# A lead-in with a written order on TensorE: modulation columns amid the products, modulation weights loaded ahead of x, products of zeros first

## The chip, the core and the metric

The kernel runs on one core of a Trainium2 chip. The metric is the device time of one execution in microseconds. A time is given as the median of several executions, and a profile shows one execution of its own. The engines are named as in the profile: PE is TensorE (matrix products), PEld its weight loads, DVE is VectorE, ACT is ScalarE, POOL is GpSimd, and SP is the engine that issues most of the transfers from memory.

## What is computed

One inference step of a two-layer trunk for 512 latent tokens (`x_sample`) and 128 context tokens (`x_prompt`), each a row of 1024 features. Layer 0 is gated attention with grouped keys and values, layer 1 a gated linear recurrence. The change touches the start of layer 0 alone:

```python
def _adaln(cond, w, b):
    mod = silu(cond) @ w + b                  # w: 1024 x 3072
    return split(mod, 3)                      # shift, scale, gate

# layer 0, for the context tokens (cond = c_ctx) and the latent tokens (cond = c)
sh, sc, g = _adaln(cond, ada_w[0], ada_b[0])
h = x * (1.0 + sc) + sh                       # the modulated tokens
proj = h @ attn_w_in                          # q, k, v and the gate path
...
out = attention(q, k, v) * silu(gate) @ attn_w_out
x = layer_norm(ALPHA * x + g * out)
```

So before the first product of a feature's rows of `attn_w_in` can run, three things are wanted: that feature of x with features on the partitions (a transpose), its shift and scale (a small product with 1 MB of `ada_w` for 128 features), and the weights.

## The kernel before

All products are float32 made of three products in a faster format: an operand is split into a high part (a rounded copy, made by ACT) and a low part (the rest, made by DVE), and high x high, high x low and low x high are added up in PSUM. In the names, `hhi` and `hlo` are the parts of the modulated tokens, `kvhi` and `kvlo` those of the key and value columns of `attn_w_in`, and `whi` and `wlo` those of other weights.

The lead-in handles the 1024 features as eight feature tiles of 128, which the text numbers 0 to 7, and the 640 tokens as five token tiles. For one feature tile the steps are:

- **Transposes** (`flip`, lines 440 to 450): TensorE turns x for two feature tiles at once, in ten transposes into three PSUM banks (`xps`, 4, 4 and 2 of them); DVE, ACT and DVE copy them to `h32`.
- **Modulation columns** (`ada_feat`, line 279): 16 products of silu(cond) with two 512 KB pieces of `ada_w` (`raw<-in_ada_m`), eight with each piece, into `adaps`. DVE copies the sum to `row` (line 292), two tiny products on TensorE (`ada_feat_out`, line 286) turn it onto the partitions, and DVE adds the bias, which gives `shsc` (line 287).
- **Modulation** (`modulate`, lines 452 to 458): DVE scales and shifts `h32` (line 455, two instructions), ACT makes `hhi` (line 457), and DVE makes `hlo` (line 458).
- **Key and value products** (`kv_mms`, lines 474 to 476): 15 products of 512 columns, three for each token tile, added up over all eight feature tiles in five PSUM banks (`acc`). Their weights come in four pieces of 512 KB for two feature tiles each (`raw<-in_attn_kv`), which ACT and DVE split (lines 224 and 225).

After the lead-in, 120 products of 256 columns make the first queries (`pmm`, lines 337 to 339), and then the gate path begins (`gps`, line 330). Everything up to the end of attention lies in one scheduled block: a planner with an instruction timeline of its own sets the order of each engine's instructions from the dependencies, and `pin` (`tc.keep_in_program_order`) keeps those so marked in the order in which the code is written. Before the change, `pin` holds only loads and a few others in the lead-in, so that TensorE's order is the planner's. Loads go through one list, `order`, which `pump` issues on SP's queue; the lead-in's pieces share a ring of eight buffers (`RAW_START`), and a load waits until its buffer is read out. `bank1` hands out three PSUM banks in turn, which transposes, modulation sums and the tiny products share.

## Time and profile before

| | us |
|---|---|
| median of 3 runs | 848.7 (845.87 to 850.77) |
| the profiled execution, its own time | 848.41 |
| its span, first to last instruction | 846.6 |
| TensorE busy | 813.1 |
| first gate-path product starts (end of what the change can touch directly) | 73.89 |
| TensorE idle before that point | 9.4 |

Times of rows are microseconds from the start of the span. In a row of the timeline stand the start, the length, engine, source line, operation, output<-inputs, shapes and count, and in brackets the idle time of the engine before it with what ended it. Rows of several instructions are merged, so that a row's length covers all of them. A matmul's length holds the time that it takes to leave the array, which the next one overlaps: how fast TensorE gets on is read from the starts. In a row of windows stand the stretch, its length, the busy time of each engine with the number of instructions, the granted TensorE clock as a share of full speed, the share of the 16 DMA engines that was busy, and GB/s. The time between the profiled execution's span and its time is 1.8 us.

### The profile page before, as it was taken

What the parts mean: (1) busy time and instruction counts of PE and PEld (TensorE: products, weight loads), DVE (VectorE), ACT (ScalarE), POOL (GpSimd) and SP (SyncE); (2) the same over time, 40 slices, a digit from 0 to 9 for tenths busy, and PEclk for the clock granted to TensorE, in tenths of its full rate; (3) what the DMA queues carried; (4) which work ended last, traced back from release to release, by engine and by line L of the source; (5) the groups of instructions that cost most, each with busy time, mean ns of one, the idle gap of its engine ahead of it and who ended that gap; (6) DMA issues with size and microseconds to landing.
All of it is one profiled execution on the core that took longest, in us unless ns stands there. A gap on an engine that the chain in (4) does not pass through costs nothing.

```text
span 846.6 us, 19382 instructions
## 1 busy us (share of the span) xinstructions
PE 813.1 (96%) x8144; PEld 730.3 (86%) x8144; DVE 529.0 (62%) x952; ACT 382.8 (45%) x767; POOL 213.3 (25%) x263
## 2 busy tenths in 40 slices
PE   6999998999999997999999999999999999999994
PEld 4789998878888765788999999999999999997774
DVE  3557434575657656676438575766668575858476
ACT  2232536565655766322434434445434544445232
POOL 0214002344324743110001204243333314121121
PEclk9999999999999999999999999999999999999998
DMA  9932122135152154631322323331332323324041
GB/s 337 376 103 87 51 75 76 52 125 182 51 174 76 58 170 131 202 128 54 101 75 61 96 72 95 82 108 51 107 88 82 94 66 88 119 65 157 17 165 74
DMA packets 33990, 92.50 MB, mean 109 GB/s; under 512 B 5024, under 2 KB 12208, under 8 KB 33904
## 3 DMA queue, kind: packets, MB, share of 16 engines
q1 hardware_dynamic: 22992, 72.95, 25.7%
q0 software_dynamic: 4864, 14.44, 5.7%
q10 hardware_dynamic: 6048, 3.88, 1.5%
q8 instruction: 64, 1.05, 0.5%
q14 instruction: 22, 0.18, 0.1%
HBM read 82.06 MB, written 9.19 MB: 108 GB/s over the span
## 4 chain that ended last, share of the span: by engine, by line
PE 87%; DVE 5%; DMA 3%; ACT 2%; issue 2%; POOL 0%; SPq 0%; DVEq 0%; ACTq 0%; POOLq 0%
PE rps L1198 7%; PE rps L1199 7%; PE rps L1200 7%; PE vgps L1188 5%; PE vgps L1190 5%; PE vgps L1189 5%; PE pot L790 4%; PE pt L872 3%; PE outp L1037 3%; PE outp L1039 3%; PE outp L1038 3%; PE lv L1331 2%; PE gps L330 2%; PE gps L331 2%; PE gps L332 2%; PE sc L763 2%
## 5 line engine op out<-in xcount | busy, mean ns | idle before, releaser
L1198 PE MATMUL rps<-h1hi,rhi 128*128 128x320 f32 x368 | 118.3, 321 | 0.0
L1199 PE MATMUL rps<-h1lo,rhi 128*128 128x320 f32 x368 | 113.7, 309 | 0.0
L1200 PE MATMUL rps<-h1hi,rlo 128*128 128x320 f32 x368 | 113.6, 309 | 0.0
L865 POOL TENSOR_SCALAR p<-p,rc 128x640 f32<-128x640 f32 x64 | 54.3, 852 | 125.7 <-DVE rc L864 110.3
L857 DVE TENSOR_REDUCE nm<-sc 128x1 f32<-128x640 f32 x64 | 52.1, 819 | 33.8 <-PE sc L764 33.2
L1198 PEld LDWEIGHTS rps<-h1hi,rhi 128*128 128x128 f32 x368 | 69.1, 188 | 1.3
L1199 PEld LDWEIGHTS rps<-h1lo,rhi 128*128 128x128 f32 x368 | 69.2, 188 | 0.0
L1200 PEld LDWEIGHTS rps<-h1hi,rlo 128*128 128x128 f32 x368 | 69.1, 188 | 0.0
L225 DVE TENSOR_TENSOR rlo<-raw,rhi 128x1024 fp32r<-128x1024 f32 x32 | 45.0, 1408 | 33.9 <-ACT rhi L224 33.9
L1359 POOL COPY At<-near 32x160 f32<-32x160 f32 x32 | 14.0, 439 | 197.4 <-DVE near L1321 196.4
L860 ACT ACTIVATE p<-sc,nm 128x640 f32<-128x640 f32 x64 | 51.4, 804 | 22.8 <-DVE nm L857 12.8
L224 ACT CAST rhi<-raw 128x1024 fp32r<-128x1024 f32 x32 | 33.6, 1050 | 52.1 <-PE rps L1199 48.7
L1309 ACT COPY kc<-A 128x640 f32<-128x640 f32 x40 | 32.3, 806 | 54.4 <-DVE A L1340 50.7
L872 PE MATMUL pt<-small,p 128*128 128x128 f32 x320 | 49.2, 278 | 3.6 <-ACT pts L768 1.8
L1188 PE MATMUL vgps<-rhi,h1hi 128*128 128x256 f32 x180 | 51.5, 286 | 0.0
L1189 PE MATMUL vgps<-rlo,h1hi 128*128 128x256 f32 x180 | 50.9, 283 | 0.0
L1190 PE MATMUL vgps<-rhi,h1lo 128*128 128x256 f32 x180 | 50.8, 282 | 0.0
L768 ACT COPY pts<-pt 128x512 f32<-128x512 f32 x64 | 35.9, 590 | 28.9 <-PE pt L872 28.6
L872 PEld LDWEIGHTS pt<-small,p 128*128 128x128 f32 x320 | 36.8, 140 | 12.7 <-issue 6.4
L763 PE MATMUL sc<-kk,X 128*128 128x320 f32 x128 | 43.4, 348 | 3.0 <-ACT p L860 2.8
L1188 PE MATMUL vgps<-wspare,h1hi 128*128 128x256 f32 x140 | 41.7, 298 | 0.0
L330 PE MATMUL gps<-hhi,whi 128*128 128x320 f32 x128 | 40.0, 312 | 0.4 <-ACT X L616 0.4
(290 smaller groups left out, 2385.4 us busy)
## 6 DMA issues: line engine op xcount, KB each, us to landing
raw<-in_rec_w_in SPq DMA_DIRECT2D x40, 512.0 KB, 3.8
raw<-in_ada_s SPq DMA_DIRECT2D x32, 512.0 KB, 3.9
raw<-in_ada_m SPq DMA_DIRECT2D x16, 512.0 KB, 8.5
raw<-in_attn_w_in SPq DMA_DIRECT2D x16, 512.0 KB, 4.4
raw<-in_attn_w_out SPq DMA_DIRECT2D x8, 512.0 KB, 4.2
raw<-in_rec_w_out SPq DMA_DIRECT2D x8, 512.0 KB, 3.6
x1d<-y SPq DMA_DIRECT2D x5, 512.0 KB, 2.6
rx<-x1d POOLq DMA_DIRECT2D x20, 128.0 KB, 3.2
```

The lines of the kernel that those rows point to most:

```text
L330: nc.tensor.matmul(ps[:, :320], w.hi(k)[:, c], hhi[:, k, t], start=(k == 0), stop=False)
L763: nc.tensor.matmul(out, X[:, h, t0:t0 + P], kk[:, c, k0:k1], start=True, stop=False)
L857: nc.vector.tensor_reduce(nm[:, 0:1], sc[:, :, :320], AX.XY, ALU.max, negate=True)
L860: nc.scalar.activation(halves(p[:]), sc[:, :, :320], AF.Exp, bias=nm[:, 0:1], accum_out=su[:, 0:1])
L865: nc.gpsimd.tensor_scalar(p, p, rs[:, 0:1], 1.0, ALU.mult, ALU.mult)
L872: nc.tensor.transpose(pt[:, i * 256 + q * P:i * 256 + (q + 1) * P], ps[q][:, (k0 + i) * P:(k0 + i + 1) * P], ident)
L1188: nc.tensor.matmul(out, h1hi[:, k, t], hi, start=(k == 0), stop=False)
L1189: nc.tensor.matmul(out, h1hi[:, k, t], lo, start=False, stop=False)
L1190: nc.tensor.matmul(out, h1lo[:, k, t], hi, start=False, stop=(k == KT - 1))
L1198: nc.tensor.matmul(ps[:, j, :320], hi[:, k, :], h1hi[:, k, t], start=(k == 0), stop=False)
L1199: nc.tensor.matmul(ps[:, j, :320], hi[:, k, :], h1lo[:, k, t], start=False, stop=False)
L1200: nc.tensor.matmul(ps[:, j, :320], lo[:, k, :], h1hi[:, k, t], start=False, stop=(k == KT - 1))
```

## The change

Nothing is computed otherwise; the change orders the lead-in anew.

- **Loads.** The small constants (`small`: the identity, silu's input, the biases) are issued first on SP's queue, no longer on ACT's. The first two modulation pieces come next, then half of the first key and value piece (features of tile 0), then x for the first two feature tiles, then the other half (tile 1). The halves take a buffer of the ring each. From the second pair of feature tiles on the order of loads is the old one.
- **ACT's table.** A silu of one zero stands ahead of the silu of the conditioning vector, so that the function table is loaded before `small` has landed.
- **Products of zeros** (`WARM`): 8 products of 512 columns on a tile of zeros at the very start, 2 more after the first modulation columns, and 3 more after the first transposes. Their result is overwritten.
- **Tile 0** (`first_tiles`): DVE scales and shifts straight from PSUM, in three pieces; ACT makes `hhi` in three pieces.
- **TensorE's order is written out.** `pin` now marks every transpose, modulation product, tiny product and key and value product of the lead-in. For tile ft the order is: the modulation columns of tile ft+1 (and, for odd ft, the transposes of the next pair), six products of tile ft, the tiny products of tile ft+1, and the other nine products of tile ft. The modulation of tile ft+1 stands amid the nine.
- **Order on ACT and DVE.** Splits of weights are issued only after the copies of transposes or the `hhi` and `hlo` that stand in `late`.

```diff
+WARM = (8, 2, 3)
...
-    nc.scalar.dma_start(small, a["small"])
+    nc.sync.dma_start(small, a["small"])
...
+    nc.scalar.activation(sil[:, 0, 2:3], sil[:, 0, 2:3], AF.Silu)
     nc.scalar.activation(sil[:, :, 0:2], cond, AF.Silu)
...
-        order.append(("x", c4))
-        order.extend(lead)
-        order.append(("attn_kv", 0, c4))
+        if c4:
+            order.append(("x", c4))
+            order.extend(lead)
+            order.append(("attn_kv", 0, c4))
+        else:
+            order.extend(lead)
+            order.extend((("kvh", 0, 0), ("x", 0), ("kvh", 0, 1)))
         order.extend(("ada_m", part * KT + 2 * c4 + 1, 0) for part in range(2))
...
+        def first_tiles():
+            pa, pb, pc = (bank1("xps") for _ in range(3))
+            for i in range(TS):
+                turn_x(pa[:, i * P:(i + 1) * P], 0, i)
+            for f in range(2):
+                turn_x(pb[:, f * P:(f + 1) * P], f, TS)
+            for i in range(TS):
+                turn_x(pc[:, i * P:(i + 1) * P], 1, i)
+            for c, src in ((slice(0, CW), pa[:, :CW]), (slice(CW, 512), pa[:, CW:]), (slice(512, NT), pb[:, :P])):
+                shift_scale(0, c, src)
+                late[:] = [nc.scalar.copy(hhi[:, 0, c], h32[:, 0, c]).ins]
+            late.append(nc.vector.tensor_copy(h32[:, 1, 512:], pb[:, P:2 * P]).ins)
+            nc.vector.tensor_tensor(hlo[:, 0, :], h32[:, 0, :], hhi[:, 0, :].bitcast(F32), ALU.subtract)
+            with tc.issue_after(late[0]):
+                nc.scalar.copy(h32[:, 1, :512], pc)
...
+        def warm(n):
+            for _ in range(n):
+                pin(nc.tensor.matmul(acc[TS], zero[:, :P], zero, start=True, stop=True))
...
-        for ft in range(KT):
-            if ft % 2 == 0:
-                flip(ft // 2)
-            ps = bank1("adaps")
-            ada_feat(ps, ft)
-            row = ada_row(ps)
-            if ft % 2 == 0:
-                kv_split(ft // 2)
-            if ft:
-                kv_mms(ft - 1)
-            ada_feat_out(ft, row)
-            modulate(ft)
+        warm(WARM[0])
+        row = ada_begin(0)
+        split = kv_split(0)
+        warm(WARM[1])
+        late.append(ada_feat_out(0, row))
+        next(split)
+        first_tiles()
+        warm(WARM[2])
+        drain(split)
+        for tt in range(TT):
+            kv_mm(0, tt, 0)
+        row = ada_begin(1)
+        for tt in range(TT):
+            kv_mm(0, tt, 1)
+        ada_feat_out(1, row)
+        modulate(1)
+        for tt in range(TT):
+            kv_mm(0, tt, 2)
+        for ft in range(1, KT):
+            if ft < KT - 1:
+                row = ada_begin(ft + 1)
+            if ft % 2 and ft < KT - 1:
+                flip(ft // 2 + 1)
+                drain(kv_split(ft // 2 + 1))
+            if ft == KT - 1:
+                break
+            kv_mms(ft, range(2))
+            ada_feat_out(ft + 1, row)
+            modulate(ft + 1)
+            kv_mms(ft, range(2, TT))
...
-        first_w = Weights("attn_w_in", 0, LEAD_LO)
-        kv_mms(KT - 1)
+        first_w = Weights("attn_w_in", 0, LEAD_LO, late)
+        kv_mms(KT - 1, range(TT))
```

The first place is the start of TensorE's list, before (`sil` is silu(cond), `acc_161` to `acc_165` are the five token tiles):

```order
L448 MATMUL xps<-small,xt 128x128 x10
L279 MATMUL adaps<-raw,sil 32x128 x16
L286 MATMUL adaps_216<-small,row 128x2 x2
L279 MATMUL adaps<-raw,sil 32x128 x8
L474 MATMUL acc_161<-kvhi,hhi 128x512
L474 MATMUL acc_162<-kvhi,hhi 128x512
L474 MATMUL acc_163<-kvhi,hhi 128x512
```

The same place after the change, where `acc_163` to `acc_167` are the token tiles:

```order
L506 MATMUL acc_167<-hlo 128x512 x8
L287 MATMUL adaps<-raw,sil 32x128 x16
L506 MATMUL acc_167<-hlo 128x512 x2
L294 MATMUL adaps_201<-small,row 128x2 x2
L459 MATMUL xps<-small,xt 128x128 x10
L506 MATMUL acc_167<-hlo 128x512 x3
L523 MATMUL acc_163<-kvhi,hhi 128x512
L523 MATMUL acc_164<-kvhi,hhi 128x512
```

The transposes have moved behind the modulation columns of tile 0, and 13 products of zeros (line 506) stand around them.

The second place is TensorE's list in the middle of the lead-in, from the last product of tile 3 on, before:

```order
L476 MATMUL acc_165<-kvhi,hlo 128x512
L286 MATMUL adaps_444<-small,row 128x2 x2
L279 MATMUL adaps<-raw,sil 32x128 x16
L286 MATMUL adaps_486<-small,row 128x2 x2
L448 MATMUL xps<-small,xt 128x128 x8
L474 MATMUL acc_161<-kvhi,hhi 128x512
```

After the change, from the last product of tile 2 to the tiny products of tile 4:

```order
L523 MATMUL acc_167<-kvhi,hlo 128x512
L287 MATMUL adaps<-raw,sil 32x128 x16
L523 MATMUL acc_163<-kvhi,hhi 128x512
L523 MATMUL acc_163<-kvlo,hhi 128x512
L523 MATMUL acc_163<-kvhi,hlo 128x512
L523 MATMUL acc_164<-kvhi,hhi 128x512
L523 MATMUL acc_164<-kvlo,hhi 128x512
L523 MATMUL acc_164<-kvhi,hlo 128x512
L294 MATMUL adaps_390<-small,row 128x2 x2
L523 MATMUL acc_165<-kvhi,hhi 128x512
```

Before, the tiny products followed right behind the modulation columns from which DVE has first to copy `row`; now six products stand between the two, and nine behind them.

The third place is DVE's list where a pair of feature tiles has been transposed, before (modulation of tile 3, the copy of a transposed pair, the split of a weight piece):

```order
L287 TENSOR_TENSOR shsc_78<-adaps_378,small 128x2x2
L450 COPY h_140<-xps 128x2x256
L455 TENSOR_SCALAR h_140<-h_140,shsc_78 128x512
L455 TENSOR_SCALAR h_140<-h_140,shsc_78 128x128
L225 TENSOR_TENSOR kvlo<-raw,kvhi 128x1024
L458 TENSOR_TENSOR hlo<-h_140,hhi 128x640
```

After the change, the modulation of tile 2:

```order
L468 COPY h_141<-xps 128x2x256
L468 COPY h_141<-xps 128x2x128
L233 TENSOR_TENSOR kvlo<-raw,kvhi 128x1024
L295 TENSOR_TENSOR shsc_79<-adaps_344,small 128x2x2
L472 TENSOR_SCALAR h_141<-h_141,shsc_79 128x512
L472 TENSOR_SCALAR h_141<-h_141,shsc_79 128x128
L480 TENSOR_TENSOR hlo<-h_141,hhi 128x640
```

Both copies and the split of the weights now stand ahead of the modulation at such a place.

More of the change, by code (lines that the diff above doesn't have):

```diff
@@ L220, in split_piece @@
         assert got == src, (got, src)
+        raw = raw[:, :hi.shape[-1]]
         with ExitStack() as st:
@@ L460, in hybrid_step @@
+        zero = hlo[:, KT - 1, :512]
+        nc.vector.memset(zero.bitcast(F32), 0.0)
         pump()
@@ L478, in hybrid_step, with kv_mm @@
-        for ft in range(KT):
-            if ft % 2 == 0:
-                flip(ft // 2)
+            if i == 0:
+                for n in range(2):
+                    c = slice(n * 512, (n + 1) * 512)
+                    split_piece(hi[:, c], lo[:, c], ("kvh", 0, n), nc.vector, late)
+                    yield
+            else:
+                split_piece(hi, lo, ("attn_kv", 0, i), LEAD_LO[i % 2], late)
+            wkv.append((hi, lo))
+        def kv_mm(ft, tt, n):
+            w = wkv[ft // 2][n == 1][:, ft % 2 * 512:(ft % 2 + 1) * 512]
+            x = (hhi, hhi, hlo)[n][:, ft, tt * P:(tt + 1) * P]
+            pin(nc.tensor.matmul(acc[tt], x, w, start=(ft == 0 and n == 0), stop=(ft == KT - 1 and n == 2)))
```

55 lines of the change are left out of this document (32 added, 23 removed).

## The prediction

> **What bounds the kernel now.** I read the page's busy times first, then TensorE's timeline up to the first gate-path product.
>
> ```profile
> PE 813.1 (96%) x8144; PEld 730.3 (86%) x8144; DVE 529.0 (62%) x952; ACT 382.8 (45%) x767; POOL 213.3 (25%) x263
> ```
>
> TensorE is busy for 96% of the span, so what shortens or lengthens TensorE's list reaches the end almost one to one. The change edits only the lead-in; behind it TensorE keeps its order but for a few rows. So the question is how much time TensorE loses before 73.89 us. TensorE's timeline:
>
> ```profile
> 5.19 2.37 PE L448 MATMUL xps<-small,xt 128*128 128x128 f32 x10 [5.19 <-DMA xt<-in_xs]
> 7.54 2.24 PE L279 MATMUL adaps<-raw,sil 128*32 128x128 f32 x32
> 10.42 0.99 PE L286 MATMUL adaps<-small,row 128*128 128x2 f32 x4 [0.64 <-DVE row L292]
> 11.37 1.08 PE L279 MATMUL adaps<-raw,sil 128*32 128x128 f32 x16
> 13.47 2.50 PE L474 MATMUL acc<-kvhi,hhi 128*128 128x512 f32 x5 [1.02 <-ACT hhi L457]
> 15.90 1.08 PE L279 MATMUL adaps<-raw,sil 128*32 128x128 f32 x16
> 16.91 1.43 PE L475 MATMUL acc<-kvlo,hhi 128*128 128x512 f32 x5
> 18.18 1.31 PE L476 MATMUL acc<-kvhi,hlo 128*128 128x512 f32 x5
> ...
> 21.52 1.08 PE L279 MATMUL adaps<-raw,sil 128*32 128x128 f32 x32 [0.54 <-DVE h L450]
> ...
> 28.15 0.61 PE L286 MATMUL adaps<-small,row 128*128 128x2 f32 x4 [0.55 <-DVE row L292]
> 28.61 1.07 PE L448 MATMUL xps<-small,xt 128*128 128x128 f32 x8
> 29.44 0.48 PE L474 MATMUL acc<-kvhi,hhi 128*128 128x512 f32 x1
> ...
> 33.01 0.38 PE L448 MATMUL xps<-small,xt 128*128 128x128 f32 x2
> 33.32 1.08 PE L279 MATMUL adaps<-raw,sil 128*32 128x128 f32 x32
> 34.33 0.51 PE L474 MATMUL acc<-kvhi,hhi 128*128 128x512 f32 x1
> ...
> 37.93 0.50 PE L286 MATMUL adaps<-small,row 128*128 128x2 f32 x4
> 38.36 1.08 PE L279 MATMUL adaps<-raw,sil 128*32 128x128 f32 x32
> 39.98 0.61 PE L286 MATMUL adaps<-small,row 128*128 128x2 f32 x4 [0.55 <-DVE row L292]
> ```
>
> ```profile
> 52.10 0.50 PE L474 MATMUL acc<-kvhi,hhi 128*128 128x512 f32 x1 [0.90 <-ACT hhi L457]
> ...
> 62.96 0.28 PE L337 MATMUL pmm<-whi,hhi 128*128 128x256 f32 x1
> ...
> 73.89 0.31 PE L330 MATMUL gps<-hhi,whi 128*128 128x320 f32 x1
> ```
>
> Three things are to be seen. First, idle time in brackets: 5.19 + 0.64 + 1.02 + 0.54 + 0.55 + 0.55 + 0.90 = 9.4 us. Second, a slow start: until 16.9 us everything takes twice as long. Five products take 2.43 us from 13.47 to 15.90, and 1.27 from 16.91 to 18.18. The excess is 1.2 in the transposes (2.35 against 0.83 + 0.31), 1.2 in the first modulation columns (2.24 against 1.01 from 33.32 to 34.33), 0.5 in the tiny products, 1.1 in the second columns and 1.2 in the five products: 5.2 us. Third, the prices of undisturbed work, from start to start: 1.01 us for a tile's modulation columns, 3.60 for its 15 products (34.33 to 37.93), 0.43 for its tiny products, 1.14 for ten transposes, and 0.119 for one `pmm` product (92 of them from 62.96 to 73.89). Eight tiles, four rounds of transposes and 120 `pmm` make 40.3 + 4.6 + 14.3 = 59.2 us, and with 9.4 and 5.2 that is 73.8 of the 73.89. So 14.6 us are lost, and no more than that is to be had.
>
> **How early can it go?** The loads bound the first stages:
>
> ```profile
> 9.98 1.04 ACT L224 CAST kvhi<-raw 128x1024 fp32r<-128x1024 f32 x1 [2.23 <-DMA raw<-in_attn_kv]
> 18.25 1.05 ACT L224 CAST kvhi<-raw 128x1024 fp32r<-128x1024 f32 x1 [4.84 <-DMA raw<-in_attn_kv]
> ```
>
> ```profile
> 35.00:40.00 5.00, 4.46 (x51) 3.60 (x49) 1.39 (x4) 0.44 (x1) 0.00 (x0) 1.00 1.00 379
> 40.00:45.00 5.00, 5.00 (x29) 4.27 (x29) 3.89 (x7) 3.12 (x5) 0.00 (x0) 1.00 0.36 143
> ```
>
> The windows show the DMA engines full until about 40 us. Both casts start when their piece lands. The first lies behind 97 + 640 + 2 x 512 + 512 = 2273 KB of issued loads, the second behind 5473 KB, so the stream brings 387 KB per us, and a load with C KB up to its own end lands at 9.98 + (C - 2273)/387.
>
> **The change, part by part.** *Loads.* The first two modulation pieces now end at 97 + 1024 = 1121 KB and land at 7.0 us (before they stood behind x); x for tiles 0 and 1 ends at 2017 KB and lands at 9.3, later than its 5.19. The pieces of tile 1 end at 3297 KB, as before: 12.6. Those of tile 2 end at 4961 KB: 16.9. Those of tile 7 end at 13217 KB: 38.3. The first stages are then a race with the loads, and nothing in tiles 0 and 1 can bring tile 2's columns to an end before 16.9 + 0.5.
>
> *ACT's table and `small`.* The table load and the move of `small` to SP's queue are costed at nothing: silu is wanted at 7.0. Before, x needed `small` at 5.19, so it is there in time even if it lands 1 us later.
>
> *Tile 0.* For the splits and the modulation I take these rows of DVE and ACT:
>
> ```profile
> 9.85 0.42 DVE L292 COPY row<-adaps 128x256 f32<-128x256 f32 x1 [1.83 <-PE adaps L279]
> 12.52 1.22 DVE L225 TENSOR_TENSOR kvlo<-raw,kvhi 128x1024 fp32r<-128x1024 f32 x1
> 13.66 0.81 DVE L458 TENSOR_TENSOR hlo<-h,hhi 128x640 fp32r<-128x640 f32 x1
> ...
> 19.87 0.16 DVE L287 TENSOR_TENSOR shsc<-adaps,small 128x4 f32<-128x4 f32 x1 [2.39 <-PE adaps L286]
> 20.07 0.80 DVE L455 TENSOR_SCALAR h<-h,shsc 128x512 f32<-128x512 f32 x2
> ```
>
> ```profile
> 12.69 0.72 ACT L457 CAST hhi<-h 128x640 fp32r<-128x640 f32 x1 [1.67 <-DVE h L455]
> ...
> 29.72 0.59 ACT L450 COPY h<-xps 128x512 f32<-128x512 f32 x1 [1.28 <-PE xps L448]
> ```
>
> At full pace the second half of tile 0's columns ends at 7.5, `row` at 8.0, the tiny products at 8.6, `shsc` at 8.8. Ahead of the modulation now stand the half cast of the weights (half of 1.04) and its low part (half of 1.22) in DVE's queue: 10.1. A piece of the modulation and a piece of `hhi`, some 0.4 each by their rows' lengths, let the first real product start at 11.1, against 13.47. Five products end at 12.3; tile 1's columns end at 12.6 + 0.5; five products, tiny products, five products take 1.3 + 0.43 + 1.3: 16.2. Tile 2's columns then end with their second piece, at 17.4. The bounds of that point are 16.9 + 0.5 and, if the first stages stay slow, the cold rival's below.
>
> *From there on TensorE's list alone counts.* Three rounds of transposes (3.4), columns of tiles 3 to 7 (5.05), six pairs of tiny products (2.6), products of tiles 1 to 7 (25.2) and 120 `pmm` (14.3): 50.5 us. The same sum for before, from 21.52, gives 50.4, and with its waits of 0.55, 0.55 and 0.90 it ends at 73.9, as measured.
>
> *The new order's own price.* The 15 products are cut in two by the tiny products. A row that follows another shape is longer by 0.12 (1.43 against 1.31); six times that is 0.7, with ends of 0 and 1.4. For tiles without transposes, `hhi` comes 0.16 + 0.80 + 0.72 and four hand-overs of some 0.08 after the tiny products, 2.0 us; nine products (2.1) and the next columns (1.0) hide that, and the 0.55 waits for `row` are gone because six products now hide the copy. Tile 7 has no columns behind the nine products: `hlo` (0.81) is then late by about 0.3. The splits of the first `whi` now come behind tile 7's `hlo`; cast and low part take 1.04 + 1.22, and 15 products of 3.6 us hide them: nothing. The 13 zero products fill waits for loads; at the slow pace eight take 3.9 us and end by about 5.5, ahead of 7.0: nothing.
>
> Sum: 17.4 + 50.5 + 0.7 + 0.3 = 68.9, against 73.89: 5.0 us less, rounded to 4.9 for hand-overs that I left out. The profiled execution's 848.41 becomes 843.5; it lies 0.3 below the median of 848.7, so the median becomes 843.8.
>
> **The clock: row and rule.** The weak term is the pace in tiles 0 and 1. The one other place where it drops:
>
> ```profile
> 136.41:139.82 3.41, 1.41 (x11) 1.00 0.42 142
> 139.82:143.23 3.41, 3.28 (x15) 0.50 0.09 19
> 334.36:337.77 3.41, 1.77 (x15) 1.00 0.00 0
> ```
>
> ```profile
> 139.95 0.64 PE L763 MATMUL sc<-kk,X 128*128 128x320 f32 x1 [2.12 <-ACT p L860]
> ```
>
> After 2.12 us of idle time, in a stretch in which TensorE was 41% busy, the granted clock is 0.50 for 3.4 us; a stretch with 52% at 334 left it whole. The start shows the other direction: transposes and modulation columns from 5.19 to 9.78 did not raise the pace, and 3.4 us of products from 13.47 on did. In the new order the zeros end at about 5.5 at the latest, and up to 10.4 come columns, two zeros, tiny products and transposes with waits of 0.4 to 0.8 between: some 45 to 60% busy. That is between the two rows. [...]
>
> **The rivals.**
>
> *Cold at the first real product.* For it: the row at 139.95, and no row shows whether products of zeros raise the pace. Against it: 52% was enough at 334. Then ten transposes from 9.3 take 2.35, three zeros 1.5, and the first real product starts at 13.1, 2.0 us late; if the pace comes only 3.4 us after that, columns and products cost 2.2 more. Of 4.9 us are left 0.7 to 2.9: 845.8 to 848.0, middle 846.9.
>
> *The modulation chain at transposes, slower.* At tiles 2, 4 and 6, between the last transpose and `hlo`, now stand a copy (0.59), the cast (1.04), `kvlo` (1.22), `shsc`, the scaling, `hhi` and `hlo` (0.16 + 0.80 + 0.72 + 0.81): 5.3 us, with hand-overs 5.8. What hides it is 15 products but for the last part, tiny products, columns and two products: 1.4 + 0.4 + 2.1 + 1.0 + 0.5 and re-entries, 5.6. It is nearly even, and each further microsecond is paid three times. To end 0.5% slower it would need 3 us at each; for it speaks that the piece for tiles 2 and 3 lands at 18.25, just when its transposes end (18.6), against it that the later two land 3 to 6 us ahead. From 3 us on it gives 853.
>
> *Tile 2 also gains elsewhere.* The cooled stretch at 139.95 costs half of 3.3 us; with another phase it is gone: 842.1.
>
> **How the numbers follow.** Warm lead-in 0.55, at 843.8 with 843.1 to 844.8 as its own range; cold 0.25; the further gain 0.08; slower 0.12. A change of 0.5%, 4.2 us, is about what a measurement of this kernel can tell from none; that boundary is 844.5, and I put 0.45 of the first case below it. So faster 0.45 + 0.08 = 0.53, within 0.35, slower 0.12. The range of 841.8 to 848.0 takes in the further gain and all of the cold case, and leaves out the slow one.
>
> **What would show it.** Right: the first real product at about 11 us, five of them in 1.3 us, tile 2's columns ending near 17.4, no wait above 0.5 us from there to the first gate-path product at about 69, and the same length from there to the end. Cold: five first products in 2.4 us. Slower: waits for `hhi` or `hlo` ahead of tiles 2, 4 and 6. I would be wrong altogether if the part behind the lead-in changed its length by more than 1 us, or if the loads came in another rhythm than 387 KB per us.

## The result

The changed kernel took 845.85 us in the median of 13 runs (842.26 to 847.70), the kernel before 848.19 in 13 runs beside them (845.87 to 850.77). The ratio is 0.9959, with a 95% interval from 0.9944 to 0.9974: 0.41% faster. The same kernel was measured twice more, beside the experiments: 0.9985 (0.9970 to 0.9999) and 0.9968 (0.9951 to 0.9984). The forecast, 843.8 of 848.7, was a ratio of 0.9942. So the direction was right, the time lies inside the range given, and the gain is 70% of the one forecast in the best of the three measurements (0.41 of 0.58%), 26 and 55% in the others. That the range holds the time is the cold rival's doing: 845.85 lies above the main case's own range (843.1 to 844.8) and at the lower end of the rival's (845.8 to 848.0), which had a chance of 0.25. By the prediction's line of 844.5 the outcome is "within", which had 0.35, and not "faster", which had 0.53.

The busy times of the page, after the change:

```profile
PE 817.6 (97%) x8157; PEld 732.2 (87%) x8157; DVE 531.3 (63%) x954; ACT 383.3 (45%) x771; POOL 211.5 (25%) x263
```

TensorE has the 13 products of zeros more, and is busy for 97% of a span of 844.1 us instead of 96% of 846.6. The profiled execution's own time is 845.85. Its TensorE timeline answers to the one shown of before. Line 506 is a product of zeros, 287 the modulation columns, 459 the transposes, 523 the key and value products:

```profile
1.76 3.78 PE L506 MATMUL acc<-hlo 128*128 128x512 f32 x8 [1.76 <-DVE hlo L499]
5.47 0.80 PE L287 MATMUL adaps<-raw,sil 128*32 128x128 f32 x16
6.49 0.64 PE L287 MATMUL adaps<-raw,sil 128*32 128x128 f32 x16 [0.21 <-DMA raw<-in_ada_m]
...
9.35 2.39 PE L459 MATMUL xps<-small,xt 128*128 128x128 f32 x10 [1.07 <-DMA xt<-in_xs]
11.40 1.52 PE L506 MATMUL acc<-hlo 128*128 128x512 f32 x3
12.76 1.32 PE L523 MATMUL acc<-kvhi,hhi 128*128 128x512 f32 x5
14.01 1.08 PE L287 MATMUL adaps<-raw,sil 128*32 128x128 f32 x32
...
17.98 1.08 PE L287 MATMUL adaps<-raw,sil 128*32 128x128 f32 x32
18.99 1.31 PE L459 MATMUL xps<-small,xt 128*128 128x128 f32 x10
...
26.35 0.50 PE L523 MATMUL acc<-kvhi,hlo 128*128 128x512 f32 x1 [0.45 <-DVE hlo L480]
...
52.85 0.50 PE L523 MATMUL acc<-kvhi,hhi 128*128 128x512 f32 x1 [0.17 <-ACT hhi L479]
...
71.10 0.31 PE L338 MATMUL gps<-hhi,whi 128*128 128x320 f32 x1
```

The first gate-path product starts at 71.10 us instead of 73.89. From there to the end of the span it is 773.0 us, and was 772.7: all of the gain is made in the lead-in. The waits of before (0.54, 0.55, 0.55, 0.90) are gone, and two small ones have come (0.45 and 0.17). But the ten transposes take 2.05 us to the next start, where 1.14 was expected, and the first real product starts at 12.76, not at 11.1. The windows show why. Columns are as in the windows of before; 1.00 or 0.50 ahead of the DMA share is the granted clock:

```profile
5.86:9.27 3.41, 2.21 (x38) 1.33 (x30) 1.22 (x3) 0.62 (x1) 0.00 (x0) 1.00 0.99 321
9.27:12.68 3.41, 3.33 (x13) 3.13 (x14) 2.00 (x5) 1.55 (x5) 0.00 (x0) 0.50 1.03 394
135.56:138.97 3.41, 1.76 (x15) 1.15 (x16) 1.40 (x4) 2.36 (x5) 0.80 (x1) 1.00 0.45 150
138.97:142.38 3.41, 3.41 (x20) 2.28 (x19) 1.44 (x6) 2.52 (x5) 1.60 (x2) 0.50 0.42 154
```

From 9.27 to 12.68 us the granted clock is 0.50: the pace had been raised behind the zeros (the second half of the first modulation columns takes 0.57 us from 6.49 to 7.06; before, the whole took 2.24), and was taken back just when x had landed. The same happens at 139 us, as it did in the profile of before.

### The profile page after: what moved, and what is told of

It is laid out like the page before. It is cut to its first block, busy times and chain, and to the rows that moved or that the text cites. A ratio compares the mean times of both kernels' runs of the same rounds, so it can differ in the third digit from the quotient of the medians.

```text
span 844.1 us, 19415 instructions
## 1 busy us (share of the span) xinstructions
PE 817.6 (97%) x8157; PEld 732.2 (87%) x8157; DVE 531.3 (63%) x954; ACT 383.3 (45%) x771; POOL 211.5 (25%) x263
## 4 chain that ended last, share of the span: by engine, by line
PE 88%; DVE 5%; ACT 2%; DMA 2%; issue 1%; POOL 0%; SPq 0%; DVEq 0%; ACTq 0%; POOLq 0%
PE rps L1273 7%; PE rps L1274 7%; PE rps L1275 7%; PE vgps L1263 5%; PE vgps L1265 5%; PE vgps L1264 5%; PE pot L865 4%; PE outp L1112 4%; PE pt L947 3%; PE outp L1114 3%; PE outp L1113 3%; PE acc L523 3%; PE lv L1406 2%; PE gps L338 2%; PE gps L339 2%; PE sc L838 2%
## 5 line engine op out<-in xcount | busy, mean ns | idle before, releaser
L932 DVE TENSOR_REDUCE nm<-sc 128x1 f32<-128x640 f32 x64 | 52.1, 819 | 33.6 <-PE sc L839 33.0
L1263 PE MATMUL vgps<-rhi,h1hi 128*128 128x256 f32 x180 | 51.5, 286 | 0.0
L865 PE MATMUL pot<-pts,vv 128*64 128x256 f32 x320 | 40.4, 398 | 1.1 <-DVE pts L843 1.1
```

What stands on the lines that cost most here:

```text
L865: nc.tensor.matmul(pot[j * HD:(j + 1) * HD, :CW], vv[:, slot, c * HD:(c + 1) * HD], moving[j], start=first, stop=last)
L932: nc.vector.tensor_reduce(nm[:, 0:1], sc[:, :, :320], AX.XY, ALU.max, negate=True)
L1263: nc.tensor.matmul(out, h1hi[:, k, t], hi, start=(k == 0), stop=False)
```

## The experiments

Theory A, after the result: the early columns carry the gain; what is missing is the pace in tiles 0 and 1. Rivals: the written order carries it; the order of loads alone does; or the pace does not matter because tile 2's pieces bound the lead-in. All kernels were timed in eleven runs or more, the kernel before in 34 or 35 beside each group; e1 to e4 share a chip, as do e5 and e7 to e9, and e10 and e12 to e14. The table gives starts in the profiled execution, in us.

| kernel | first real product | its five products take | first gate-path product | ratio to before (95%) |
|---|---|---|---|---|
| before | 13.47 | 2.43 | 73.89 | 1 |
| changed | 12.76 | 1.25 | 71.10 | 0.9959 (0.9944 to 0.9974) |
| e5, changed again | 14.06 | 1.25 | 72.75 | 0.9985 (0.9970 to 0.9999) |
| e14, changed again | 11.55 | 1.27 | 69.75 | 0.9968 (0.9951 to 0.9984) |
| e1, no zeros | 11.97 | 2.43 | 71.67 | 0.9973 (0.9959 to 0.9988) |
| e2, five more zeros | 11.55 | 1.26 | 69.96 | 0.9962 (0.9950 to 0.9975) |
| e12, e2 again | 11.57 | 1.23 | 71.56 | 0.9966 (0.9948 to 0.9984) |
| e8, e2 and late tables | 12.19 | 1.26 | 70.40 | 0.9970 (0.9956 to 0.9984) |
| e13, e2 and x ahead | 11.77 | 1.27 | 70.27 | 0.9967 (0.9951 to 0.9982) |
| e4, planner's order from tile 2 | 14.32 | 1.35 | 73.78 | 0.9979 (0.9966 to 0.9992) |
| e10, e4 without zeros | 11.72 | 2.15 | 73.95 | 0.9985 (0.9975 to 0.9996) |
| e3, old order of loads | 16.01 | 1.24 | 74.74 | 0.9998 (0.9983 to 1.0012) |
| e7, x and transposes first, zeros | 16.03 | 2.09 | 74.97 | 1.0018 (1.0007 to 1.0030) |
| e9, written order alone | 13.76 | 2.33 | 74.00 | 1.0017 (1.0006 to 1.0028) |

### e1: without the products of zeros

```diff
-WARM = (8, 2, 3)
+WARM = (0, 0, 0)
```

> The changed kernel without its 13 products of zeros (8, 2 and 3 become 0, 0 and 0), all else as it is. Theory A (the pace decides the first stages): the modulation columns, transposes and the first five real products all run at half pace, the five in about 2.4 us from about 12.5 us; the pace rises some 3.4 us after the first of them; tile 2's columns end at 20 to 21 us instead of 18.99 and the first gate-path product starts at about 72.8 instead of 71.10. Time about 847.5 us. Theory B (the first stages only race with the loads, the zeros are of no use): tile 2's columns end at about 19 and the gate path starts at 71.1 within 0.3 us, time as the changed kernel's 845.9.

```profile
9.78 2.39 PE L459 MATMUL xps<-small,xt 128*128 128x128 f32 x10 [0.80 <-DMA xt<-in_xs]
11.97 2.50 PE L523 MATMUL acc<-kvhi,hhi 128*128 128x512 f32 x5
...
71.67 0.31 PE L338 MATMUL gps<-hhi,whi 128*128 128x320 f32 x1
```

Without zeros the lead-in is slow up to 16 us, as before the change, and still the first gate-path product starts 2.2 us earlier than there. The half pace up to 16 us came as theory A had it; the gate path lies between the 72.8 of A and the 71.1 of B. Against the changed kernel's first profile the zeros are worth 0.6 us, against its third (e14, below) 1.9, and its second (e5, 72.75) is 1.1 later than e1. In time e1 lies between the three measurements of the changed kernel, so a gain by the zeros in time is not shown.

### e2 and e12: five more zeros in the wait for x

```diff
         late.append(ada_feat_out(0, row))
+        warm(5)
         next(split)
```

> The changed kernel with five more products of zeros between the tiny products of tile 0 and the first transposes, where TensorE waits 1.07 us for x and the granted clock falls to 0.50. Theory A: the clock stays at 1.00, ten transposes take 1.1 us instead of 2.05, the three zeros 0.7 instead of 1.36, the first real product starts at about 11.2 instead of 12.76, tile 2's columns end at 17.5 and the gate path starts at 69.5 to 69.8; about 1.4 us less than the changed kernel, 844.4 us. Theory B: the loads of tile 2 and the chain of tile 0 set the pace anyway and the gate path starts at 71.1 within 0.3 us.

```profile
9.70 1.31 PE L459 MATMUL xps<-small,xt 128*128 128x128 f32 x10
...
11.55 1.33 PE L523 MATMUL acc<-kvhi,hhi 128*128 128x512 f32 x5
...
17.73 0.65 PE L287 MATMUL adaps<-raw,sil 128*32 128x128 f32 x16 [0.26 <-DMA raw<-in_ada_m]
```

The pace holds: transposes in 1.06 us to the next start, the first real product at 11.55. Then TensorE waits for tile 2's second piece, and of the 1.2 us won by 11.55, 0.7 are left at the end of tile 2's columns (18.30 against 18.99). In all four profiles with the five zeros (e2, e8, e12, e13) no stretch of the lead-in cooled; without them one of three kept the pace (e14). On another chip, beside the changed kernel:

> The changed kernel with five more products of zeros in the wait for x, a second time, beside the changed kernel on the same chip. Theory A (the cooled stretch from 9.3 to 12.7 us is the part of the shortfall that can be had back): 0.8 to 1.5 us below the changed kernel here, first real product within 2.2 us of the landing of x. Rival B (the pace there does not matter, as tile 2's pieces bound the lead-in in either case): within 0.4 us of the changed kernel.

```profile
19.37 0.64 PE L287 MATMUL adaps<-raw,sil 128*32 128x128 f32 x16 [1.89 <-DMA raw<-in_ada_m]
...
71.56 0.31 PE L338 MATMUL gps<-hhi,whi 128*128 128x320 f32 x1
```

Here tile 2's piece landed 1.6 us later than in e2, and the wait of 1.89 took back what the pace had won. In time e12 and the changed kernel are the same on that chip (means of 846.05 and 845.96), so rival B is right as far as time goes: five more zeros do not beat the changed kernel by what can be measured.

### e14 and e5: the changed kernel twice more

> The changed kernel, unaltered, as the measure of the three others on this chip: expected ratio to before 0.9972 within 0.0015, between the 0.9959 and 0.9985 of its two measurements. If the time goes with the landing of x (9.35 us in the one profile, 10.83 in the other), a profile with x before 9.6 has its first gate-path product before 71.4, one with x behind 10.5 behind 72.3.

```profile
6.52 0.64 PE L287 MATMUL adaps<-raw,sil 128*32 128x128 f32 x16 [0.37 <-DMA raw<-in_ada_m]
...
9.71 1.31 PE L459 MATMUL xps<-small,xt 128*128 128x128 f32 x10 [1.38 <-DMA xt<-in_xs]
...
11.55 1.34 PE L523 MATMUL acc<-kvhi,hhi 128*128 128x512 f32 x5
...
17.73 0.64 PE L287 MATMUL adaps<-raw,sil 128*32 128x128 f32 x16 [0.24 <-DMA raw<-in_ada_m]
18.31 1.31 PE L459 MATMUL xps<-small,xt 128*128 128x128 f32 x10
...
69.75 0.31 PE L338 MATMUL gps<-hhi,whi 128*128 128x320 f32 x1
```

> The changed kernel once more, unaltered, beside the three kernels below on one chip. Theory A (the pace in tiles 0 and 1 was the step that failed: the stretch from 9.3 to 12.7 us cools because TensorE is 28% busy before x lands): the profile shows the transposes at about 9.4 in 2.4 us, five first products in 1.3 to 2.5 us, the first gate-path product at 71.1 within 0.5. Rival B (that stretch was the accident of one execution): transposes in 1.3 us, gate path at 69.5 to 70. In time both expect the ratio to before that was measured, 0.996 within 0.0015.

```profile
10.83 2.39 PE L459 MATMUL xps<-small,xt 128*128 128x128 f32 x10 [1.67 <-DMA xt<-in_xs]
...
72.75 0.31 PE L338 MATMUL gps<-hhi,whi 128*128 128x320 f32 x1
```

The same program, three executions, three lead-ins: 69.75 with the pace kept (842.74 us), 71.10 with the pace lost (845.85), 72.75 with the pace lost and x 1.5 us late (847.32). Its ratios miss the expectation of e5 (0.9985 where 0.996 within 0.0015 was expected) and meet that of e14; x landed at 9.71 in e14, between the two cases named there. For e5 the rival "accident of one execution" falls, since it cooled again; with e14 the theory that the wait for x as such cools TensorE falls as well, since e14 waited longer for x (1.38 against 1.07) and kept the pace. What goes with the loss is where the wait lies on a grid. In rows of a quarter of a microsecond (3 to 25, 130 to 150 and 325 to 342 us), every stretch of granted clock 0.50 is 3.41 us long or twice that, and within one execution all of them start at the same remainder of 3.413 us: 2.44 for the changed kernel's first profile (9.27, 138.97 and 333.53, which lie 129.70 and 194.56 us apart, 38 and 57 times 3.413), 0.10 to 0.11 for e5 (10.34, 140.05, 334.61), 2.20 for e14's only one (329.88). So in these profiles the cooled stretches lie on a grid whose phase differs from execution to execution. The windows of e14 on its grid, and that of e5 ahead of its cooled stretch:

```profile
5.61:9.03 3.42, 2.34 (x38) 1.47 (x35) 0.82 (x3) 0.62 (x1) 0.00 (x0) 1.00 0.93 282
9.03:12.44 3.41, 2.73 (x17) 2.35 (x18) 2.33 (x6) 1.42 (x5) 0.00 (x0) 1.00 1.03 405
...
131.91:135.32 3.41, 1.83 (x13) 1.58 (x12) 2.68 (x3) 3.37 (x4) 0.12 (x1) 1.00 0.32 92
135.32:138.73 3.41, 2.87 (x26) 2.10 (x30) 1.21 (x4) 2.33 (x7) 1.60 (x2) 1.00 0.34 105
```

```profile
6.93:10.34 3.41, 2.02 (x30) 1.19 (x22) 0.97 (x3) 0.62 (x1) 0.00 (x0) 1.00 1.00 332
```

In the lead-in TensorE was busy for 2.34 of 3.42 us here and the next stretch stayed whole, and for 2.21 in the first profile and 2.02 (6.93 to 10.34) in e5, where the next one cooled. The 28% in e5's expectation is the busy share of 8 to 9 us alone; over the stretch of the grid it is 65%. In the attention the same wait of 2.12 us stands in the first profile (up to 137.21) and in e14 (up to 135.86), and e5 has 2.13 us of idle time there. In e5 all of it lies in one stretch (TensorE busy for 1.28 us from 136.64 to 140.05), and the next cooled; in the first profile a boundary leaves 1.65 us of it in the second stretch (1.76 busy), and the next cooled; in e14 a boundary cuts it into 1.58 and 0.54 (1.83 and 2.87 busy), and nothing cooled. Busy time alone does not give the bound: after 1.77 of 3.41 the pace stayed at 334 in the profile of before, and after 2.21 it did not in the lead-in. Which work counts for how much was not tried, so that the cut by the grid decides is the reading that fits these rows, not one that an experiment set. The scatter of the runs, 842.3 to 847.7, is of the size of a few such stretches: a cooled one costs up to 1.7 us by estimate, half of its 3.41, since the products in the one of e10 start some 0.43 us apart (28.59 to 29.87), against 0.23 at full pace (e14, 50.72 to 50.95).

### e3: the old order of the first loads

x comes first again; TensorE's written order is left, columns ahead of transposes.

```diff
+        order.append(("x", c4))
+        order.extend(lead)
         if c4:
-            order.append(("x", c4))
-            order.extend(lead)
             order.append(("attn_kv", 0, c4))
         else:
-            order.extend(lead)
-            order.extend((("kvh", 0, 0), ("x", 0), ("kvh", 0, 1)))
+            order.extend((("kvh", 0, 0), ("kvh", 0, 1)))
```

> The changed kernel with the old order of the first loads: x for tiles 0 and 1 ahead of the first two modulation pieces (the halves of the first weight piece right behind those). Theory A (tile 2's pieces, which land at 16.9 either way, bound the first stages): modulation columns of tile 0 end at about 9.2 instead of 7.1, the wait for x is gone, the first real product starts between 12 and 13, and the gate path starts within 0.5 us of the changed kernel's 71.10. Rival (the new order of loads is what gains): each of the 1.7 us by which the modulation pieces land later is paid, gate path at about 72.8, time 1.7 us above the changed kernel's.

```profile
9.07 2.27 PE L287 MATMUL adaps<-raw,sil 128*32 128x128 f32 x32 [3.60 <-DMA raw<-in_ada_m]
```

All of the gain is gone, more than either theory had: the first real product starts at 16.01 and the gate path at 74.74. But this does not price the order of loads by itself: TensorE must now wait 3.60 us for the pieces that stand first in its order, while x lies ready, and loses the pace for two stretches (8.65 to 15.48).

### e7: x and the transposes first, with zeros in the waits

e3's order of loads, with these edits beside it:

```diff
-WARM = (8, 2, 3)
+WARM = (8, 8, 2, 7)
...
-        row = ada_begin(0)
-        split = kv_split(0)
+        flip(0)
         warm(WARM[1])
-        late.append(ada_feat_out(0, row))
-        next(split)
-        first_tiles()
+        row = ada_begin(0)
+        drain(kv_split(0))
         warm(WARM[2])
-        drain(split)
+        ada_feat_out(0, row)
+        modulate(0)
+        warm(WARM[3])
```

> The old order of the first loads (x ahead of the modulation pieces), with the transposes first in TensorE's written order, the copies to h32 and the two-instruction modulation of the kernel before for tile 0, and 8, 8, 2 and 7 products of zeros that fill the waits; from tile 1 on as after the change. Theory A (loads bound the first stages only through tile 2's pieces, which land at about 17.7 in either order; what counts is that the pace is kept and TensorE has something to do): transposes at about 5.2, first real product at 11.5 to 13, gate path at 69.8 to 71, time equal to the changed kernel's within 0.8 us. Rival B (loading the modulation pieces ahead of x is itself worth the 3.5 us that undoing it alone cost): gate path at 73 or later, time 2.5 us or more above the changed kernel's.

```profile
11.32 1.37 DVE L233 TENSOR_TENSOR kvlo<-raw,kvhi 128x512 fp32r<-128x512 f32 x2 [3.02 <-ACT kvhi L232]
12.61 0.42 DVE L300 COPY row<-adaps 128x256 f32<-128x256 f32 x1
```

Slower than before by 0.18%. The transposes ran at 5.56 as meant, but on DVE both low parts of the weights came ahead of `row`, TensorE waited 1.80 us for it, the clock fell to half behind that wait (14.46 to 17.86), and the first real product came at 16.03. By its numbers rival B came true (gate path at 74.97), but the kernel made a new wait and tells the two theories apart only in part: theory A's 11.5 to 13 us was not reached, and products of zeros do not make up for a chain on DVE.

### e9: the written order alone

As e7, with no zeros, `small` on ACT's queue and no early table load:

```diff
-WARM = (8, 2, 3)
+WARM = (0, 0, 0, 0)
...
-    nc.sync.dma_start(small, a["small"])
+    nc.scalar.dma_start(small, a["small"])
...
-    nc.scalar.activation(sil[:, 0, 2:3], sil[:, 0, 2:3], AF.Silu)
```

> Only TensorE's written order for tiles 1 to 7 (columns, six products, tiny products, nine products) with the order of splits on ACT and DVE; the old first loads, the transposes first, no products of zeros, no early table load, the old modulation of tile 0. Theory A (the written order takes away the waits of 0.54, 0.55, 0.55 and 0.90 us behind tile 1 and nothing else): the first real product at about 13.5 as before, gate path at 71.4 to 72.2, time 1.5 to 2.5 us below before, ratio 0.997 to 0.998. Rival B (the new order is worth nothing without the early start): gate path at 73 to 74, ratio 0.9995 to 1.0005.

```profile
13.76 2.40 PE L521 MATMUL acc<-kvhi,hhi 128*128 128x512 f32 x5 [2.25 <-ACT hhi L477]
...
20.62 1.08 PE L286 MATMUL adaps<-raw,sil 128*32 128x128 f32 x32
...
74.00 0.31 PE L337 MATMUL gps<-hhi,whi 128*128 128x320 f32 x1
```

Rival B was right: alone, the written order is worth nothing, rather 0.2% less. The waits of 0.55 are gone, but tile 1's columns no longer stand in the first wait (2.25 instead of 1.02), and the stretch after that wait is cooled, 13.89 to 17.30. The row of before at which the same work is left (three rounds of transposes, the columns of tiles 2 to 7, the products of tiles 1 to 7 and the first queries):

```profile
19.69 1.29 PE L448 MATMUL xps<-small,xt 128*128 128x128 f32 x10
```

From there to the gate path are 54.2 us before, and 53.4 from 20.62 in e9. So the written order wins 0.8 us behind tile 0's products, and e9 lost 0.9 ahead of that point; what it is slower beyond that lies behind the gate path's start (774.3 us against 772.7 in these executions).

### e4 and e10: the planner's order from tile 2 on, with and without zeros

```diff
+        listed[0] = False
+        for ft in range(2, KT):
+            if ft % 2 == 0:
+                flip(ft // 2)
+            row = ada_begin(ft)
+            late[:] = []
+            if ft % 2 == 0:
+                drain(kv_split(ft // 2))
+            kv_mms(ft - 1, range(TT))
+            ada_feat_out(ft, row)
+            modulate(ft)
+        late[:] = []
```

This loop takes the place of the changed kernel's, and `listed` switches `pin` off for TensorE's instructions; e10 has no zeros as well.

> The changed kernel with TensorE's order for feature tiles 2 to 7 left to the planner again, in the old loop and without the rule that splits come behind late copies; tiles 0 and 1, the loads and the zeros as in the changed kernel. Theory A (the written order is worth the waits that it hides): waits for row of 0.55 us come back at two tiles, with waits of 0.5 to 0.9 for a modulation chain; 2 to 2.5 us of idle time between tile 2 and the gate path, which starts at about 72.9; time 1.5 to 2 us above the changed kernel's. Rival (the written order only moves the waits): gate path at 71.1 within 0.4 us.

> The new order of the first loads, the early table load and the new form of tile 0 and of the first products of tile 1 alone: no products of zeros, and from tile 2 on TensorE's order is the planner's as before the change. Theory A (the early columns carry the gain, the written order from tile 2 on is worth nothing, as it was alone): the first real product starts at 11.9 to 13, about a us ahead of before, and the first gate-path product at 72.2 to 73.2; ratio to before 0.9975 to 0.9985, within 1 us of the changed kernel without zeros. Rival B (the written order and the early columns pay only together): gate path at 73.5 or later, ratio 0.999 to 1.001.

```profile
11.72 2.21 PE L527 MATMUL acc<-kvhi,hhi 128*128 128x512 f32 x5
...
17.75 1.25 PE L463 MATMUL xps<-small,xt 128*128 128x128 f32 x10
...
26.28 0.61 PE L298 MATMUL adaps<-small,row 128*128 128x2 f32 x4 [1.26 <-DVE row L304]
...
52.17 0.50 PE L527 MATMUL acc<-kvhi,hhi 128*128 128x512 f32 x1 [1.22 <-ACT hhi L483]
...
73.95 0.31 PE L342 MATMUL gps<-hhi,whi 128*128 128x320 f32 x1
```

In e10 the first real product is 1.75 us ahead of before's, by the loads, the early table load, the new form of tile 0 and the order written out for tiles 0 and 1. In this execution that is lost again by tile 7: the planner's order waits 1.26, 0.55 and 1.22 us, and one stretch cooled from 27 us on (products some 0.43 us apart from 28.59 to 29.87). For the work that takes 54.2 us before (above), e10 takes 56.2 (17.75 to 73.95, of which the cooled stretch is 1.7 by the estimate above) and e4 54.2 (19.55 to 73.78); with the written order it is 53.1 in the first profile (17.98 to 71.10), 53.5 in e5 (19.27 to 72.75) and 52.9 in e14 (16.84 to 69.75). In time e10 is 0.15% faster than before, e4 0.21%; by the ratios e4 is 0.7 us above the mean of the changed kernel's three, where theory A had 1.5 to 2. The written order, on top of the early start, adds some 0.1% (e1 against e10, and the mean of the changed kernel's three ratios, 0.9971, against e4), no more than half the intervals' width. So the early start has 0.15 to 0.21% and the written order some 0.1%, and the intervals do not tell which is the larger part. How much of the early start is the order of loads and how much the new form of tile 0 stays open, since the runs that undo only one of the two (e3 and e7) made new waits.

### e13: x ahead of the half piece

```diff
-            order.extend((("kvh", 0, 0), ("x", 0), ("kvh", 0, 1)))
+            order.extend((("x", 0), ("kvh", 0, 0), ("kvh", 0, 1)))
...
```

It is e2 otherwise, except that the first half's low part comes behind tile 0's modulation on DVE.

> The kernel with five more zeros, and x issued ahead of the first half of the key and value piece, whose low part DVE now makes behind tile 0's modulation. Theory A (tile 2's second piece bounds the lead-in once the pace is kept; x only sets when the first stages start): x lands some 0.7 us earlier, the first real product starts at 10.7 to 11.3, but the wait for tile 2's second piece grows from 0.3 to 0.8 to 1.3 us and the first gate-path product stays within 0.3 us of the kernel with five more zeros; time equal within 0.4 us. Rival B (the first stages themselves bound it): gate path 0.6 us earlier or more. Both expect the hole in the load stream, 124 to 178 GB/s around 6 to 7 us, to move about 0.7 us forward if it belongs to x.

```profile
18.08 0.64 PE L295 MATMUL adaps<-raw,sil 128*32 128x128 f32 x16 [0.31 <-DMA raw<-in_ada_m]
```

x landed some 0.9 us earlier than in e2 (8.8 against 9.7, from issue and time to landing). The transposes, at 9.98, no longer wait for it, but the five zeros ahead of them ended only then, so the first real product came no earlier (11.77). Tile 2's columns wait for their piece again, but 0.31 us and not the 0.8 to 1.3 expected, as nothing ahead of them had been won. The first gate-path product, at 70.27, is within 0.3 us of e2's, as theory A had it. The expectation for the hole in the load stream failed: it moved back, to 253 and 232 GB/s from 7 to 9 us. So these rows do not tie it to x.

### e8: POOL's tables behind tile 7

```diff
+        gone = tiny.tile([P, 1], F32, tag="gone", name="gone")
+        pin(nc.gpsimd.tensor_copy(gone, hlo[:, KT - 1, :1].bitcast(F32)))
-        nc.gpsimd.tensor_scalar(qg, qg, 1.0 / math.sqrt(HD), 1.0, ALU.mult, ALU.mult)
+        pin(nc.gpsimd.tensor_scalar(qg, qg, 1.0 / math.sqrt(HD), 1.0, ALU.mult, ALU.mult))
```

The four table products behind it are pinned too; the five zeros of e2 stay.

> Five more products of zeros in the wait for x, and POOL's rotary tables held back until tile 7's low part is made. Theory A (DVE's modulation of tile 3 took 1.30 instead of 0.80 us because POOL ran tensor work at the same moment): the two instructions of tile 3's modulation take 0.80, its low part 0.82, the 0.45 us wait ahead of the product at 26 is gone, gate path at about 69.5 against 69.96 with the zeros alone. Rival B (DVE is slow there for another reason): the wait stays, gate path at 70.0. In time against the changed kernel: A and B both expect 0 to 1.5 us less, since the lead-in no longer cools.

The changed kernel's first profile on DVE and POOL at tile 3, then e8's DVE:

```profile
23.02 1.30 DVE L472 TENSOR_SCALAR h<-h,shsc 128x512 f32<-128x512 f32 x2
25.17 1.13 DVE L480 TENSOR_TENSOR hlo<-h,hhi 128x640 fp32r<-128x640 f32 x1 [0.85 <-ACT hhi L479]
```

```profile
23.36 0.86 POOL L567 TENSOR_TENSOR cosk<-rope,kg 128x256 f32<-128x256 f32 x1
...
25.57 1.32 POOL L567 TENSOR_TENSOR sinq<-rope,qg 128x256 f32<-128x256 f32 x1
```

```profile
22.98 0.80 DVE L472 TENSOR_SCALAR h<-h,shsc 128x512 f32<-128x512 f32 x2
24.64 0.83 DVE L480 TENSOR_TENSOR hlo<-h,hhi 128x640 fp32r<-128x640 f32 x1 [0.85 <-ACT hhi L479]
```

With POOL still, the two steps take 0.80 and 0.83 us instead of 1.30 and 1.13, so POOL's work at the same moment made them longer, and made the wait of 0.45 at 26.35. In time e8 and e2 cannot be told apart: the wait was a small one, and in e2 only the second step was hit (1.15 us). Beside the changed kernel on its chip (e5), e8 is 1.4 us lower in the mean (845.46 against 846.85), with an interval of 1.3 us either way; A and B both allow that, and e12, which has the five zeros alone, showed no such gain.

## Where the prediction was right and where it failed

- **The bound and the neutral rest: right.** What the lead-in lost was the gain; from the first gate-path product on the length is 773.0 us against 772.7.
- **The sum behind tile 2's columns: right.** It was 50.5 + 0.7 + 0.3 = 51.5 us. Measured, from the end of those columns to the first gate-path product: 51.4 in e14 (18.31 to 69.75), 52.1 in the first profile (18.99 to 71.10), in which one product (26.35) starts 0.6 us late behind the wait of 0.45. The waits for `row` are gone as it said. The small terms were not measured one by one, and tile 7 cost more than its 0.3: in e14 two starts there (51.50 and 52.36) each come 0.3 us later than the product before them would let them, so the total is right in part by terms that make up for one another.
- **The clock in tiles 0 and 1: the step that failed.** The prediction named it the weak term and put 0.55 on "the pace holds" and 0.25 on "cold", as two ways of which one would be true of the kernel. Both are true of it, by execution. The zeros do raise the pace (half a tile's columns in 0.57 us, where the whole took 2.24 before), which no row of before could show; that it would then hold was the author's estimate. The first profile and e5 lost it and e14 kept it, and by the reading of the windows above that goes with how the thin work up to the landing of x falls on the grid. The prediction set that work, 45 to 60% busy, between its rows of 41% (cooled) and 52% (not); on the grid it was 65% and cooled, so the busy share on which it weighed the two cases was not the measure. Where it held (e14), the forecast of the first real product was 0.45 us early (11.1, measured 11.55), and where it was lost, 1.7 (12.76) and 3.0 (14.06 in e5, where x also landed 1.5 us late). The cold rival's 13.1 us and middle of 846.9 come near to the profiles with the pace lost (12.76 and 845.85; 14.06 and 847.32).
- **The load law: too exact.** For x, 9.3 was forecast and 9.35, 9.71 and 10.83 measured in three executions. Tile 2's second piece was forecast at 16.9; it landed at 17.73 in e14 and e2, and at 19.37 in e12. As the columns end 0.5 to 0.6 us behind it, this bound was 0.9 us late even in the best lead-in; in the first profile, where the piece landed at 17.3, the lost pace and not the piece set the start of the columns (17.98). The law had one execution behind it. The move of `small` and the early table load, which the prediction put at nothing, go with a hole in the load stream (below), but e9, which has neither, got the same piece only at 17.6, against 16.9 before (from issue and time to landing). So why it is late stays open. With 18.3 in place of 17.4, the same sum gives 69.8; e14 measured 69.75.
- **The further gain: right in mechanism.** Pace kept in the lead-in and no cooled stretch at 139 was put at 842.1 with a chance of 0.08; e14 is that execution, at 842.74. By the same reading it goes with the phase of the grid, which was 2.44, 0.10 and 2.20 us in three executions of the same program.
- **The chain at the transposes: rightly ranked as unlikely.** The largest wait there in the first profile is 0.45 us, and its cause is POOL, which the prediction had left out; in e5 two of 0.31 and 0.42 stand there.
- **The written order: the size fits, the time does not show it.** The sum gave it 2.0 us of waits less 1.0 of price. For the same work behind tile 0's products the three profiles of the changed kernel show 0.7 to 1.3 us less than before (53.5 to 52.9 against 54.2). In time it is some 0.1%, 1 us, on top of the early start, which the intervals do not tell from none; alone it brings nothing (e9), where the longer wait at the start takes back what the middle wins.

Together, for the first profile: 5.0 us forecast, 2.8 measured. Of the 2.2 us, 1.6 were lost by the end of tile 2's columns (18.99 against 17.4), in which the lost pace and the later loads overlap, and 0.6 behind it. The three measurements of the ratio put the gain at 0.15, 0.32 and 0.41%, and their intervals reach from 0.01 to 0.56%.

## What to carry to other kernels

Where TensorE waits for loads at the start, order the loads so that each piece that lands finds work that wants no other piece; the early start as a whole, of which this is part, brought 0.15 to 0.21% here, and writing out TensorE's order brought nothing without it. A forecast that hangs on the clock should be made as a mixture over executions: lay the 3.41 us grid of these profiles over the waits at several phases, see how much of a wait falls into one stretch, and take several profiles, as no bound for a safe stretch came out of these. Where an early stage is made faster, name the next load that bounds it, with the scatter of its landing over several profiles, before counting the gain.

## What the runs showed that was not expected

- **The cooled stretches stand on a grid** of 3.413 us with one phase for each execution (remainders of 2.44 three times in the first profile, 0.10 to 0.11 three times in e5). At the same wait of 2.1 us the next stretch cooled in two of the three profiles of the changed kernel and not in the third, where a boundary cut the wait into 1.58 and 0.54.
- **The column of the granted clock says 1.00 at the start of a span, though the pace is half.** Ten transposes take 2.35 us to the next start there (5.19 to 7.54, before) and 1.14 later, and the column is 1.00 for 0 to 9 us (first row below). The pace must be read from the starts.
- **A hole in the load stream.** The whole of 0 to 9 us of before, of e9 and of e14, each from its own windows:

```profile
0.00:9.00 9.00, 3.73 (x34) 2.94 (x38) 1.65 (x6) 2.08 (x3) 0.41 (x5) 1.00 0.74 260
```

```profile
0.00:9.00 9.00, 3.36 (x26) 2.65 (x26) 2.14 (x7) 2.08 (x3) 0.41 (x5) 1.00 0.77 256
```

```profile
0.00:9.00 9.00, 6.19 (x46) 4.09 (x46) 1.81 (x8) 2.32 (x4) 0.42 (x5) 1.00 0.74 241
```

  By 9 us before had moved 2.34 MB, e9 2.30, e14 2.17 and e7 2.06 (229 GB/s). In the kernels with `small` on SP's queue and the early table load the stream falls, somewhere between 4 and 9 us, to 124 to 232 GB/s in its lowest microsecond; in the two without these edits (before and e9) it stays above 320 from 5 to 12 us. e7 and e9 issue the same loads in the same order but for `small`. The zeros are not needed for it: e1 and e10 have none, and fall to 127 and 139 GB/s. Which of the two edits opens the hole was not tried.
- **POOL makes DVE slower.** 0.80 us became 1.30 and 0.82 (before, 22.85) became 1.13 where POOL worked at the same time; in e8, with POOL still, they are 0.80 and 0.83. It can fall on both engines: in e2 DVE's low part took 1.15 us from 23.99 on, and POOL's `sink` beside it (24.42) 1.31, where its three other tables took 0.73 or 0.74. Why both get slower was not tried.
